# One bias table with reversed queries, table transfers on GpSimd's queue, and six raw weight tiles in a two-layer decoder trunk

## The chip, the cores and the metric

The kernel runs on one core of a Trainium2 chip. The engines are TensorE (PE; its weight loads are PEld), VectorE (DVE), ScalarE (ACT), GpSimd (POOL) and SyncE (SP), each of which works through its own list of instructions in order. The metric is the device time of one execution in microseconds (us), as the median of several.

## What is computed

A trunk of two layers on 256 tokens of 1024 channels, all in float32. The first layer mixes tokens by differential attention, the second by a diagonal state space model (SSM) with a gated output. Around each mixer stand two half-weighted feed-forward parts (FFN), and at the end a gated embedding (PLE). Every part has a norm in front and one behind.

```python
def reference(x, p, norm_g, ...):
    for i in range(DEPTH):
        g = norm_g[i]
        x = x + 0.5 * rmsnorm(swiglu(rmsnorm(x, g[0]), ffn_w_in[i, 0], ffn_w_out[i, 0]), g[1])
        h = rmsnorm(x, g[2])
        if i % 2 == 0:
            m = diff_attention(h, ..., rel_bias, lambda_init)
        else:
            m = s5_glu(h, ...)
        x = x + rmsnorm(m, g[3])
        x = x + 0.5 * rmsnorm(swiglu(rmsnorm(x, g[4]), ffn_w_in[i, 1], ffn_w_out[i, 1]), g[5])
        gate = sigmoid(rmsnorm(x, g[6]) @ ple_w_gate[i])
        x = x + rmsnorm(gate * (p[i] @ ple_w_proj[i]), g[7])
    return x

# in diff_attention, for a block of 128 queries and all keys:
    dist = q_pos[:, None] - k_pos[None, :]
    bias = rel_bias[t5_bucket(dist)]              # one value per softmax map and distance
    s = einsum('bhmqd,bhmkd->bhmqk', q_blk, k) + bias
    s = where(dist >= 0, s, NEG_INF)
    prob = softmax(s)
    attn = prob[:, :, 0] - lam * prob[:, :, 1]
```

## The kernel before

The 256 tokens are two blocks of 128, each a thread of Python generators whose steps alternate (block 0 leads by some steps). All weights are streamed once: 332 tiles of 128 x 1024 floats (512 KB) go from DRAM to a "raw" slot. ScalarE rounds a raw tile to float32r (hi, L131), VectorE takes the rest (lo, L133), and each product is three float32r matmuls (L302 to L304). The class `Weights` issues the loads on SyncE's queue (L119); a raw slot comes free once lo is done, and a pair of hi and lo once both blocks have used it. There are three raw slots and nine pairs (NB).

The order of each engine's list is written by the framework's scheduler, which goes by priorities and its own estimates. The calls `high_priority` and `issue_after` steer it, and the numbers in `OPT` say where.

Early in the program the attention bias is prepared (L525 to L540). A table of 16 softmax maps by 384 distances is filled by GpSimd and written to DRAM 128 times, once for each query of a block, by eight DMAs on SyncE's queue (L539). A read whose row stride is one less than a copy (L581) gives each query its own shift.

From the end of attention on, tables for the SSM are made between the other work, in eight groups gp (L908 to L948). GpSimd forms products vr, vi and or, oi (L897 to L902). TensorE transposes and multiplies them (v_ps, m_ps and m2_ps, L923 to L936), and SyncE stores them to v_d and o_d. The last parts are the diagonal terms db and dg (L952 to L959), the Toeplitz rows in m_d (L961) and their copy in t_d from DRAM to DRAM (L964, L965), all on SyncE's queue. GpSimd also computes the norms' factors: v is the sum of squares and r its power of -1/2 (L313 to L317). In names of norms the last digit is the block: r_pnple01 is the post norm of the first layer's PLE for block 1, and r_pre101 the norm in front of the second layer's first FFN for that block.

Of the kernel before, what the change touches and what calls it, by code (L numbers as in the profile page):

```python
# [9 lines left out]
F32 = mybir.dt.float32  # L10
# [6 lines left out]
P = 128  # L17
# [5 lines left out]
# Places in the schedule, by layer (f01: block 0, second ffn) or by norm (block, norm, token half).  # L23
# [49 lines left out]
def bucket_ranges(n_buckets=32, max_dist=128, n=256):  # L73
    """[start, stop) of the distances in each causal T5 bucket."""
    exact = n_buckets // 2
    of = []
    for d in range(n):
        if d < exact:
            of.append(d)
        else:  # L80
            large = exact + int(math.log(d / exact) / math.log(max_dist / exact) * (n_buckets - exact))
            of.append(min(large, n_buckets - 1))
    return [(of.index(b), n - of[::-1].index(b)) for b in range(n_buckets)]


class Weights:
    """Streams weight tiles [128, 1024] from DRAM and splits each into two float32r parts, or takes two tiles unsplit."""

    def __init__(self, nc, raw_pool, split_pool, specs):
# [8 lines left out]
        self.raws = 3  # L98
# [24 lines left out]
    def flush(self, force):  # L123
        """Splits what is loaded, up to the limit."""
        nc = self.nc
# [17 lines left out]
def trunk(ctx, tc, x, p, norm_g, ffn_w_in, ffn_w_out, attn_w_qkv, attn_w_o, attn_lam, attn_subln_g,  # L143
# [5 lines left out]
    raw_pool = ctx.enter_context(tc.tile_pool(name="raw", bufs=3))  # L149
# [11 lines left out]
    def extra_banks(name):  # L161
        """The last two banks serve one section after another."""
# [130 lines left out]
    def after_transposes(b, key, left):  # L293
        """The second block's last products of a layer leave room for the first block's transposes of the next."""
# [67 lines left out]
    def post_norm(b, halves, gain, factor, name):  # L362
        """x += factor * rmsnorm(m) with m in two [128, 512] PSUM banks."""
# [28 lines left out]
    def two_halves(b, accs, hi, lo, units, key):  # L392
        """Products over k into both halves; the last units finish the first half before the second."""
# [122 lines left out]
    if any(st[0] == "attn" for st in stages):  # L516
# [7 lines left out]
        # bias of every softmax map by j = key - query + 127 (distance 255 - j), masked beyond 255  # L524
# [11 lines left out]
        # one copy per query: a stride of one less than a copy then shifts the table by the query  # L536
        tab_d = dram.tile([P, 16, 384], F32, name="tab_d")
        for j in range(8):
            nc.sync.dma_start(tab_d[16 * j:16 * j + 16].rearrange("r m j -> m r j"),  # L539
                              tab.rearrange("m (o j) -> m o j", o=1).broadcast_to([16, 16, 384]))  # L540
# [34 lines left out]
    def scores(b, h):  # L575
# [4 lines left out]
        src = tab_d[0, 2 * h:2 * h + 2, 127 + 256 - nk:127 + 256 - nk + 1]  # L580
        nc.sync.dma_start(bias[:, :, 0:nk], bass.AP(tensor=src.tensor, offset=src.offset,  # L581
                                                      ap=[[16 * 384 - 1, P], [384, 2], [1, nk]]))
# [34 lines left out]
    def attention(b, qkv_units, pj_units, o_units):  # L617
# [9 lines left out]
        def normed(grp, on):  # L627
# [11 lines left out]
            for h in range(4):  # L639
                nc.tensor.transpose(pt[:, h * P:(h + 1) * P], on[:, h, :], ident)  # L640
            split_T(pt, oT_hi[:, grp * 4:grp * 4 + 4, :].rearrange("p a t -> p (a t)"),
                    oT_lo[:, grp * 4:grp * 4 + 4, :].rearrange("p a t -> p (a t)"), sub_g)
# [8 lines left out]
        for n, (part, grp) in enumerate(QKV_ORDER):  # L651
# [21 lines left out]
            if part == 0:  # L673
                for m in range(2):
                    (nc.vector.tensor_copy if m >= OPT["qz"] else nc.scalar.copy)(
                        qz[b][64 * m:64 * m + 64, :, m, :], ptv[64 * m:64 * m + 64])
# [41 lines left out]
    def exact_exp(out_, in_, n, nm):  # L718
        """exp to float32 accuracy: 2^(m / 16) times a short series of the rest."""
# [14 lines left out]
    def ssm_exp():  # L734
        """lambda, lambda * dt and the moduli |a|^k with states (e, p) on partitions, columns (q, g'): group 16q + 2g' + e."""
# [20 lines left out]
    def ssm_tables(pool, keep):  # L756
# [7 lines left out]
        # sine and cosine of lambda_im * dt: reduced to [-pi, pi], polynomials of the half angle  # L764
# [24 lines left out]
        # powers of a = rho e^(i theta), then of the phase and of the modulus by squaring  # L789
# [16 lines left out]
        # phases of a^(8j), moduli of a^8  # L806
# [23 lines left out]
        # (a - 1) / lambda  # L830
# [23 lines left out]
        # the norm's gain of the input channels goes into b and d  # L854
# [11 lines left out]
        # output matrices with states on partitions  # L866
# [39 lines left out]
        nc.sync.dma_start(m_d[:, :, 0:7, :].rearrange("i g k o -> i g (k o)"),  # L906
# [42 lines left out]
        # skip connection on the diagonal, Toeplitz rows to DRAM behind seven zero blocks  # L949
        m16 = msb.rearrange("p g e q h -> p (g e q) h")  # L950
        for q in range(4):
            db = pool.tile([16, 16, 16], F32, tag="cn", name=f"db{q}", bufs=1)  # L952
            nc.sync.dma_start(db, ssm_d[:, 256 * q:256 * q + 256].rearrange("o (g h) -> o g h", h=16).broadcast_to([16, 16, 16]))
            dg = pool.tile([16, 16, 16], F32, tag="vi", name=f"dg{q}", bufs=1)
            nc.sync.dma_start(dg, norm_g[1, 2:3, 256 * q:256 * q + 256].rearrange("o (g h) -> o g h", h=16).broadcast_to([16, 16, 16]))
# [5 lines left out]
        for k in range(8):  # L961
            nc.sync.dma_start(m_d[:, :, 7 + k, :], m16[16 * k:16 * k + 16])
        yield 2
        for s_ in range(8):  # L964
            nc.sync.dma_start(t_d[16 * s_:16 * s_ + 16].rearrange("i g (c x) -> i (g c) x", x=P),  # L965
# [4 lines left out]
    def ssm_u(b):  # L970
        """x and the norm's factors to the layout (channel group, block) x (step, channel) through DRAM."""
# [35 lines left out]
    def ssm_core(pool, vs, tos):  # L1007
# [35 lines left out]
        def grouped(out_ap, st_, w, **flags):  # L1043
            """One product per channel group: 32 stationary columns and 128 moving columns each."""
# [288 lines left out]
```

## Time and profile before

| What | Value |
|---|---|
| median of 3 runs | 1148.12 us (1147.39 to 1149.25) |
| profiled execution, span from its first to its last instruction | 1145.0 us |
| what lies around the span (median less span) | 3.1 us |
| TensorE busy | 1049.3 us, 92% |
| VectorE / ScalarE / GpSimd busy | 694.8 / 554.4 / 241.3 us |
| moved by DMA | 221.74 MB, mean 194 GB/s |

Times are of one profiled execution. A line as L131 is line 131 of the kernel before. Busy time of TensorE is modelled at its end and includes pipelining, so the number of its instructions in a window tells more of its pace than the share of time. A wait is put down to what came last.

### The profile page before, as it was taken

What the parts mean: (1) busy time and instruction counts of PE and PEld (TensorE: products, weight loads), DVE (VectorE), ACT (ScalarE), POOL (GpSimd) and SP (SyncE); (2) the same over time, 40 slices, a digit from 0 to 9 for tenths busy, and PEclk for the clock granted to TensorE, in tenths of its full rate; (3) what the DMA queues carried; (4) which work ended last, traced back from release to release, by engine and by line L of the source; (5) the groups of instructions that cost most, each with busy time, mean ns of one, the idle gap of its engine ahead of it and who ended that gap; (6) DMA issues with size and microseconds to landing.
All of it is one profiled execution on the core that took longest, in us unless ns stands there. A gap on an engine that the chain in (4) does not pass through costs nothing.

```text
span 1145.0 us, 14323 instructions
## 1 busy us (share of the span) xinstructions
PE 1049.3 (92%) x5123; PEld 839.2 (73%) x5123; DVE 694.8 (61%) x1011; ACT 554.4 (48%) x873; POOL 241.3 (21%) x289
## 2 busy tenths in 40 slices
PE   6599999999998999999787997999966999999997
PEld 4478888878776787777665776888744878888885
DVE  5166554659838897555678563655358576555464
ACT  5255444556765544443455542544343465444454
POOL 6000000000012004888889400000122010000001
PEclk9799999999999999999998998999987999999999
DMA  8976655646439667666556579756693557564651
GB/s 219 163 246 210 186 189 192 200 145 211 157 128 207 181 192 203 202 206 223 176 165 198 142 204 308 236 200 208 207 358 137 172 178 220 184 186 170 211 168 56
DMA packets 138103, 221.74 MB, mean 194 GB/s; under 512 B 34352, under 2 KB 63024, under 8 KB 138032
## 3 DMA queue, kind: packets, MB, share of 16 engines
q1 hardware_dynamic: 136976, 220.17, 62.8%
q8 instruction: 40, 0.66, 0.2%
q10 hardware_dynamic: 1056, 0.66, 0.2%
q14 instruction: 31, 0.25, 0.1%
HBM read 205.13 MB, written 19.86 MB: 196 GB/s over the span
## 4 chain that ended last, share of the span: by engine, by line
PE 48%; issue 19%; POOL 11%; DMA 9%; DVE 6%; ACT 4%; SPq 3%; DVEq 0%; POOLq 0%; ACTq 0%
PE up L302 7%; PE up L303 7%; PE up L304 7%; DMA raw<-in_ffn_w_in_dram 5%; PE dn L304 4%; PE dn L302 4%; PE dn L303 4%; DVE lo L133 2%; PE qkvat L302 2%; PE qkvat L303 2%; PE qkvat L304 2%; ACT hi L131 2%; POOL or L899 1%; PE sp L586 1%; DMA db<-in_ssm_d_dram 1%
## 5 line engine op out<-in xcount | busy, mean ns | idle before, releaser
L133 DVE TENSOR_TENSOR lo<-raw,hi 128x1024 fp32r<-128x1024 f32 x332 | 425.0, 1286 | 292.3 <-ACT hi L131 289.7
L131 ACT CAST hi<-raw 128x1024 fp32r<-128x1024 f32 x332 | 347.7, 1051 | 349.0 <-DMA raw<-in_ffn_w_in_dram 121.0
L302 PE MATMUL up<-hi,xThi 128*128 128x512 f32 x704 | 281.7, 403 | 22.5 <-ACT sg L444 8.9
L303 PE MATMUL up<-lo,xThi 128*128 128x512 f32 x704 | 280.3, 400 | 2.4 <-DVE lo L133 2.4
L304 PE MATMUL up<-hi,xTlo 128*128 128x512 f32 x704 | 281.6, 405 | 0.0
L302 PEld LDWEIGHTS up<-hi,xThi 128*128 128x128 f32 x704 | 135.5, 193 | 52.8 <-ACT sg L444 9.8
L303 PEld LDWEIGHTS up<-lo,xThi 128*128 128x128 f32 x704 | 135.3, 192 | 33.0 <-DVE lo L133 5.0
L304 PEld LDWEIGHTS up<-hi,xTlo 128*128 128x128 f32 x704 | 135.1, 193 | 29.2 <-issue 0.8
L302 PE MATMUL dn<-hi,hThi 128*128 128x512 f32 x352 | 138.3, 394 | 0.0
L304 PE MATMUL dn<-hi,hTlo 128*128 128x512 f32 x352 | 138.1, 393 | 0.0
L303 PE MATMUL dn<-lo,hThi 128*128 128x512 f32 x352 | 138.0, 392 | 0.0
L313 POOL TENSOR_SCALAR v_pn<-sspn,sspn 128x1 f32<-128x1 f32 x8 | 3.4, 423 | 359.9 <-ACT junkpn L370 356.9
L304 PEld LDWEIGHTS dn<-hi,hTlo 128*128 128x128 f32 x352 | 66.4, 189 | 14.1 <-issue 0.4
L303 PEld LDWEIGHTS dn<-lo,hThi 128*128 128x128 f32 x352 | 66.4, 189 | 13.9 <-DVE lo L133 0.2
L302 PEld LDWEIGHTS dn<-hi,hThi 128*128 128x128 f32 x352 | 66.4, 189 | 13.6 <-issue 0.2
L321 ACT ACTIVATE xThi<-xT_ps,gT 128x128 fp32r<-128x128 f32 x112 | 38.9, 366 | 48.7 <-PE xT_ps L339 48.4
L326 DVE TENSOR_TENSOR hTlo<-hT_ps,hThi 128x512 fp32r<-128x512 f32 (+1 forms) x48 | 30.8, 643 | 36.6 <-ACT hThi L325 36.6
L325 ACT CAST hThi<-hT_ps 128x512 fp32r<-128x512 f32 (+1 forms) x48 | 26.4, 549 | 53.2 <-PE hT_ps L449 53.1
L322 DVE SCALAR_TENSOR_TENSOR xTlo<-xT_ps,gT,xThi 128x128 fp32r<-128x128 f32 x112 | 36.5, 344 | 20.5 <-ACT xThi L321 20.2
L339 PE MATMUL xT_ps<-ident,x 128*128 128x128 f32 x112 | 31.1, 300 | 17.7 <-DVE xTlo L322 10.7
L444 ACT ACTIVATE sg<-up,r_pre 128x512 f32<-128x512 f32 (+1 forms) x48 | 30.8, 650 | 20.9 <-PE up L304 11.5
L446 DVE SCALAR_TENSOR_TENSOR h<-up,r_pre,sg 128x512 f32<-128x512 f32 (+1 forms) x48 | 33.6, 701 | 11.0 <-ACT sg L444 8.5
(352 smaller groups left out, 1296.4 us busy)
## 6 DMA issues: line engine op xcount, KB each, us to landing
raw<-in_ffn_w_in_dram SPq DMA_DIRECT2D x160, 512.0 KB, 4.4
raw<-in_ffn_w_out_dram SPq DMA_DIRECT2D x88, 512.0 KB, 3.9
raw<-in_attn_w_qkv_dram SPq DMA_DIRECT2D x24, 512.0 KB, 4.3
raw<-in_ffn_w_in_dram SPq DMA_DIRECT2D x32, 256.0 KB, 3.5
raw<-in_ple_w_gate_dram SPq DMA_DIRECT2D x16, 512.0 KB, 4.3
raw<-in_ssm_w_glu_dram SPq DMA_DIRECT2D x16, 512.0 KB, 4.2
gain<-in_norm_g_dram SPq DMA_DIRECT2D x8, 512.0 KB, 4.8
raw<-in_attn_w_o_dram SPq DMA_DIRECT2D x8, 512.0 KB, 4.0
```

The lines of the kernel that those rows point to most:

```text
L131: nc.scalar.copy(hi, raw)
L133: (nc.gpsimd if n in self.on_pool else nc.vector).tensor_tensor(lo, raw, hi.bitcast(F32), ALU.subtract)
L302: nc.tensor.matmul(out_ap, st_hi, w_hi, start=start, stop=False)
L303: nc.tensor.matmul(out_ap, st_hi, w_lo, start=False, stop=False)
L304: nc.tensor.matmul(out_ap, st_lo, w_hi, start=False, stop=stop)
L321: return (nc.scalar.activation(hi, psum, AF.Copy, scale=scale).ins, nc.vector.scalar_tensor_tensor(lo, psum, scale, hi.bitcast(F32), ALU.m ...
L322: nc.vector.scalar_tensor_tensor(lo, psum, scale, hi.bitcast(F32), ALU.mult, ALU.subtract).ins)
L325: nc.scalar.copy(hi, psum)
L326: nc.vector.tensor_tensor(lo, psum, hi.bitcast(F32), ALU.subtract)
L339: marks[b].append(nc.tensor.transpose(pt, xb[:, k * P:(k + 1) * P], ident).ins)
L444: nc.scalar.activation(sg[:, :w], gp, AF.Silu, scale=r)
L446: nc.vector.scalar_tensor_tensor(h[:, :w], up_, r, sg[:, :w], ALU.mult, ALU.mult)
```

## The change

There are four parts. The bias table is written to DRAM once, by a DMA on GpSimd's queue. Queries are reversed when they are copied out of PSUM (query 127 comes first), so that a row stride of plus one in that single table gives each query its shift; the attention output is turned back where it is split for the next product. The zero blocks of m_d, the diagonal terms db and dg, the rows of m_d and the copies to t_d are issued by GpSimd and no longer by SyncE. The raw slots are six in place of three, and the limit on loads that wait for their split goes with them. The scratch that the framework reserves for DMA descriptors is 4096 bytes of a partition, which makes room for three more slots of 4096 bytes.

Comment lines are left out too, so line numbers from L25 to L540 are one higher in the changed kernel, and those from about L541 on one lower.

```diff
+RAWS = 6
...
-        self.raws = 3
+        self.raws = RAWS
...
-    raw_pool = ctx.enter_context(tc.tile_pool(name="raw", bufs=3))
+    raw_pool = ctx.enter_context(tc.tile_pool(name="raw", bufs=RAWS))
...
-        tab_d = dram.tile([P, 16, 384], F32, name="tab_d")
-        for j in range(8):
-            nc.sync.dma_start(tab_d[16 * j:16 * j + 16].rearrange("r m j -> m r j"),
-                              tab.rearrange("m (o j) -> m o j", o=1).broadcast_to([16, 16, 384]))
+
+        tab_d = dram.tile([16, 384], F32, name="tab_d")
+        nc.gpsimd.dma_start(tab_d, tab)
...
-        src = tab_d[0, 2 * h:2 * h + 2, 127 + 256 - nk:127 + 256 - nk + 1]
+        src = tab_d[2 * h:2 * h + 2, 256 - nk:256 - nk + 1]
         nc.sync.dma_start(bias[:, :, 0:nk], bass.AP(tensor=src.tensor, offset=src.offset,
-                                                      ap=[[16 * 384 - 1, P], [384, 2], [1, nk]]))
+                                                      ap=[[1, P], [384, 2], [1, nk]]))
...
-            split_T(pt, oT_hi[:, grp * 4:grp * 4 + 4, :].rearrange("p a t -> p (a t)"),
-                    oT_lo[:, grp * 4:grp * 4 + 4, :].rearrange("p a t -> p (a t)"), sub_g)
+            split_T(pt.rearrange("p (a t) -> p a t", a=4)[:, :, ::-1], oT_hi[:, grp * 4:grp * 4 + 4, :],
+                    oT_lo[:, grp * 4:grp * 4 + 4, :], sub_g)
...
-                        qz[b][64 * m:64 * m + 64, :, m, :], ptv[64 * m:64 * m + 64])
+                        qz[b][64 * m:64 * m + 64, :, m, :], ptv[64 * m:64 * m + 64, :, ::-1])
...
-        nc.sync.dma_start(m_d[:, :, 0:7, :].rearrange("i g k o -> i g (k o)"),
+        nc.gpsimd.dma_start(m_d[:, :, 0:7, :].rearrange("i g k o -> i g (k o)"),
...
-            nc.sync.dma_start(db, ssm_d[:, 256 * q:256 * q + 256].rearrange("o (g h) -> o g h", h=16).broadcast_to([16, 16, 16]))
+            nc.gpsimd.dma_start(db, ssm_d[:, 256 * q:256 * q + 256].rearrange("o (g h) -> o g h", h=16).broadcast_to([16, 16, 16]))
...
-            nc.sync.dma_start(m_d[:, :, 7 + k, :], m16[16 * k:16 * k + 16])
+            nc.gpsimd.dma_start(m_d[:, :, 7 + k, :], m16[16 * k:16 * k + 16])
...
-            nc.sync.dma_start(t_d[16 * s_:16 * s_ + 16].rearrange("i g (c x) -> i (g c) x", x=P),
+            nc.gpsimd.dma_start(t_d[16 * s_:16 * s_ + 16].rearrange("i g (c x) -> i (g c) x", x=P),
...
-    nc = _bacc.Bacc("TRN2", target_bir_lowering=False, num_devices=1)
+    nc = _bacc.Bacc("TRN2", target_bir_lowering=False, num_devices=1, dynamic_dma_scratch_size=4096)
```

Three places show how the lists move. In names, the first digits behind "raw" are the weight tile's number, and the last number is a buffer's.

SyncE's list in the first FFN, before: the eight writes of the table (L539) stand between the weight tiles 6 to 9.

```order
L359 DMA gain01_1251<-in_norm_g_dram 128x1024
L119 DMA raw3_290<-in_ffn_w_in_dram 128x2x512
L119 DMA raw4_296<-in_ffn_w_in_dram 128x2x512
L119 DMA raw5_302<-in_ffn_w_in_dram 128x2x512
L119 DMA raw6_308<-in_ffn_w_in_dram 128x2x512
L539 DMA tab_d_172<-tab_138 16x16x384 x3
L119 DMA raw7_314<-in_ffn_w_in_dram 128x2x512
L539 DMA tab_d_172<-tab_138 16x16x384 x2
L119 DMA raw8_320<-in_ffn_w_in_dram 128x2x512
L539 DMA tab_d_172<-tab_138 16x16x384 x3
```

The same stretch after the change:

```order
L120 DMA raw5_295<-in_ffn_w_in_dram 128x2x512
L541 DMA lam_b_174<-in_attn_lam_dram 128x256
L553 DMA sub_g_185<-in_attn_subln_g_dram 128x1
L360 DMA gain01_1244<-in_norm_g_dram 128x1024
L120 DMA raw6_301<-in_ffn_w_in_dram 128x2x512
L120 DMA raw7_307<-in_ffn_w_in_dram 128x2x512
L120 DMA raw8_313<-in_ffn_w_in_dram 128x2x512
L120 DMA raw9_400<-in_ffn_w_in_dram 128x2x512
L120 DMA raw10_418<-in_ffn_w_in_dram 128x2x512
L120 DMA raw11_436<-in_ffn_w_in_dram 128x2x512
```

The table's writes are gone from it, and tile 5 is loaded ahead of the first gain.

GpSimd's list around block 1's post norm of the first layer's PLE, before: r_pnple01 comes one product after v_pnple01.

```order
L898 TENSOR_TENSOR ptv7_4827<-ai_3143,bi_3630 128x512
L313 TENSOR_SCALAR v_pnple01_5624<-sspnple010_5618,sspnple011_5621 128x1
L897 TENSOR_TENSOR vr7_4825<-ar_3142,br_3629 128x512
L317 TENSOR_TENSOR r_pnple01_5626<-v_pnple01_5624,neg_half_92 128x1
L900 TENSOR_TENSOR vi7_4826<-ai_3143,br_3629 128x512
L899 TENSOR_TENSOR vr7_4825<-vr7_4825,ptv7_4827 128x512
L901 TENSOR_TENSOR ptv7_4827<-ar_3142,bi_3630 128x512
L315 TENSOR_SCALAR v_pre101_5661<-ss101_5659 128x1
L902 TENSOR_TENSOR vi7_4826<-vi7_4826,ptv7_4827 128x512
L317 TENSOR_TENSOR r_pre101_5663<-v_pre101_5661,neg_half_92 128x1
```

After the change, with the transfers in it:

```order
L901 TENSOR_TENSOR oi7_4898<-oi7_4898,pto7_4899 128x512
L952 DMA db0_4946<-in_ssm_d_dram 16x256
L314 TENSOR_SCALAR v_pnple01_5617<-sspnple010_5611,sspnple011_5614 128x1
L961 DMA m_d_106<-msb_3809 1024x1x16 x7
L318 TENSOR_TENSOR r_pnple01_5619<-v_pnple01_5617,neg_half_92 128x1
L954 DMA dg0_4948<-in_norm_g_dram 16x256
L954 DMA dg1_4955<-in_norm_g_dram 16x256
L316 TENSOR_SCALAR v_pre101_5654<-ss101_5652 128x1
L952 DMA db1_4953<-in_ssm_d_dram 16x256
L318 TENSOR_TENSOR r_pre101_5656<-v_pre101_5654,neg_half_92 128x1
L954 DMA dg2_4962<-in_norm_g_dram 16x256
```

Between v_pnple01 and r_pnple01 there are now seven writes of m_d, of 1024 pieces each, and the loads of dg and db stand around v_pre101.

TensorE's list where the last group of tables (v_ps70, m_ps7) begins, before: block 1's x has been transposed in part (xT_ps1010), and the second layer's first FFN (up) is under way.

```order
L304 MATMUL up10000_5520<-hi177_5523,xTlo100_5484 128x512
L304 MATMUL up10001_5593<-hi181_5596,xTlo100_5484 128x512
L339 MATMUL xT_ps1010_5632<-ident_87,x1_96 128x128
L302 MATMUL up10000_5520<-hi177_5523,xThi100_5483 128x512
L303 MATMUL up10000_5520<-lo177_5524,xThi100_5483 128x512
L302 MATMUL up10001_5593<-hi181_5596,xThi100_5483 128x512
L303 MATMUL up10001_5593<-lo181_5597,xThi100_5483 128x512
L339 MATMUL xT_ps1011_5633<-ident_87,x1_96 128x128
L304 MATMUL up10000_5520<-hi177_5523,xTlo100_5484 128x512
L304 MATMUL up10001_5593<-hi181_5596,xTlo100_5484 128x512
L923 MATMUL v_ps70_4839<-ident_87,vr7_4825 128x128
L930 MATMUL m_ps7_4854<-vr7_4825,cp0_3817 32x128 x4
```

After the change:

```order
L303 MATMUL gtple010_5386<-hi171_5290,xThi061_5351 128x512
L304 MATMUL gtple010_5386<-lo171_5291,xThi061_5351 128x512
L303 MATMUL gtple011_5387<-hi171_5290,xThi061_5351 128x512
L304 MATMUL gtple011_5387<-lo171_5291,xThi061_5351 128x512
L922 MATMUL v_ps70_4832<-ident_87,vr7_4818 128x128
L929 MATMUL m_ps7_4847<-vr7_4818,cp0_3810 32x128 x4
L340 MATMUL xT_ps0611_5354<-ident_87,x1_96 128x128
L305 MATMUL gtple010_5386<-hi171_5290,xTlo061_5352 128x512
L305 MATMUL gtple011_5387<-hi171_5290,xTlo061_5352 128x512
L340 MATMUL xT_ps1000_5478<-ident_87,x0_94 128x128
L922 MATMUL v_ps70_4832<-ident_87,vi7_4819 128x128
L922 MATMUL v_ps70_4832<-ident_87,vr7_4818 128x128
```

The last group is now among the PLE's products (gtple) of block 1, ahead of block 1's transposes. From the first v_ps50 to m2_ps7 there are 189 rows, where there were 271, and from m2_ps7 to the first xT_ps1010 there are 29 rows, 26 of them matmuls and 3 transposes.

## Rows read from the trace of the kernel before

**Rows 1.** Page, busy time by engine, then the chain that ended last:

```profile
PE 1049.3 (92%) x5123; PEld 839.2 (73%) x5123; DVE 694.8 (61%) x1011; ACT 554.4 (48%) x873; POOL 241.3 (21%) x289
...
PE 48%; issue 19%; POOL 11%; DMA 9%; DVE 6%; ACT 4%; SPq 3%; DVEq 0%; POOLq 0%; ACTq 0%
```

**Rows 2.** Windows: start:end, length, busy per engine (xinstructions), clock, DMA share, GB/s:

```profile
0.00:25.00 25.00, 15.72 (x57) 10.43 (x58) 15.00 (x44) 14.20 (x27) 14.01 (x54) 1.00 0.79 236
25.00:100.00 75.00, 59.65 (x244) 47.61 (x243) 32.50 (x39) 29.91 (x35) 3.87 (x1) 0.86 0.84 204
100.00:225.00 125.00, 125.00 (x569) 103.26 (x567) 69.16 (x69) 58.06 (x70) 0.86 (x2) 1.00 0.60 190
350.00:375.00 25.00, 20.93 (x89) 14.87 (x88) 19.98 (x69) 12.08 (x25) 5.06 (x9) 0.93 0.92 200
450.00:550.00 100.00, 93.72 (x487) 73.03 (x486) 55.02 (x44) 43.94 (x59) 86.48 (x66) 1.00 0.67 211
650.00:725.00 75.00, 65.78 (x284) 52.45 (x283) 36.19 (x44) 28.26 (x34) 1.33 (x2) 0.95 0.82 243
```

**Rows 3.** Waits, 0 to 100 us: us in total, times, longest:

```profile
ACT hi L131 <- DMA raw<-in_ffn_w_in_dram: 37.0, 21, 10.2
```

**Rows 4.** Timeline of SyncE's queue: start, duration of the issues, what:

```profile
20.21 4.22 SPq L539 DMA_DIRECT2D tab_d<-tab  x3
...
28.37 7.70 SPq L539 DMA_DIRECT2D tab_d<-tab  x2
...
36.88 8.28 SPq L539 DMA_DIRECT2D tab_d<-tab  x3
```

**Rows 5.** Windows, work on the raw weight tiles alone:

```profile
25.00:50.00 25.00, 2.45 (x2) 2.10 (x2) 0.83 0.91 138
50.00:75.00 25.00, 10.97 (x9) 9.45 (x9) 0.82 0.85 242
75.00:100.00 25.00, 12.28 (x11) 11.22 (x11) 0.93 0.75 231
100.00:225.00 125.00, 55.48 (x46) 47.49 (x46) 1.00 0.60 190
```

**Rows 6.** Issues by line (last: median us to landing), and page groups (last busy, mean ns):

```profile
raw<-in_ffn_w_in_dram SPq DMA_DIRECT2D x160, 512.0 KB, 4.4
...
L133 DVE TENSOR_TENSOR lo<-raw,hi 128x1024 fp32r<-128x1024 f32 x332 | 425.0, 1286 | 292.3 <-ACT hi L131 289.7
L131 ACT CAST hi<-raw 128x1024 fp32r<-128x1024 f32 x332 | 347.7, 1051 | 349.0 <-DMA raw<-in_ffn_w_in_dram 121.0
```

**Rows 7.** Waits, 340 to 380 us:

```profile
ACT hi L131 <- DMA raw<-in_ffn_w_in_dram: 8.0, 4, 4.2
```

**Rows 8.** SyncE's queue, 650 to 700 us:

```profile
652.05 3.49 SPq L962 DMA_DIRECT2D m_d<-msb  x4
...
684.17 11.52 SPq L965 DMA_DIRECT2D t_d<-m_d  x8
```

**Rows 9.** Chain of waits, 655 to 705 us: start, us, what:

```profile
671.20 3.54 DMA db<-in_ssm_d_dram
...
695.78 7.91 DMA raw<-in_ffn_w_in_dram
```

**Rows 10.** DMA queues, kinds, MB, share of 16 engines:

```profile
q1 hardware_dynamic: 136976, 220.17, 62.8%
q8 instruction: 40, 0.66, 0.2%
q10 hardware_dynamic: 1056, 0.66, 0.2%
```

**Rows 11.** TensorE timeline, first table transposes of groups 1 and 5, last of group 7:

```profile
470.72 0.33 PE L923 MATMUL v_ps<-ident,vr 128*128 128x128 f32 x1 [0.43 <-POOL vr L899]
...
571.48 0.27 PE L923 MATMUL v_ps<-ident,vr 128*128 128x128 f32 x1
...
646.78 0.27 PE L936 MATMUL m_ps<-ident,mt 128*128 128x128 f32 x1
```

More of the change, by code (lines that the diff above doesn't have):

```diff
@@ L952, in ssm_tables @@
             db = pool.tile([16, 16, 16], F32, tag="cn", name=f"db{q}", bufs=1)
-            nc.sync.dma_start(db, ssm_d[:, 256 * q:256 * q + 256].rearrange("o (g h) -> o g h", h=16).broadcast_to([16, 16, 16]))
+            nc.gpsimd.dma_start(db, ssm_d[:, 256 * q:256 * q + 256].rearrange("o (g h) -> o g h", h=16).broadcast_to([16, 16, 16]))
             dg = pool.tile([16, 16, 16], F32, tag="vi", name=f"dg{q}", bufs=1)
-            nc.sync.dma_start(dg, norm_g[1, 2:3, 256 * q:256 * q + 256].rearrange("o (g h) -> o g h", h=16).broadcast_to([16, 16, 16]))
+            nc.gpsimd.dma_start(dg, norm_g[1, 2:3, 256 * q:256 * q + 256].rearrange("o (g h) -> o g h", h=16).broadcast_to([16, 16, 16]))
             v.tensor_tensor(db, db, dg, ALU.mult)
```

## The prediction

> **What bounds the kernel now.** I read the busy shares and the chain first. The reader is to see that TensorE is busy in 92% of the span and leads the chain of waits with 48%, while the chain's next parts are issue time, POOL (GpSimd) with 11% and DMA with 9% [rows 1]. So what can be won is the time in which TensorE has nothing to do, and the next view is the table of windows [rows 2]. From 100 to 225 us TensorE runs 569 matrix instructions in 125 us, 4.55 per us, without a pause: that is the pace to which I hold the rest. From 25 to 100 us there are 244 where the pace allows 341, so 97 are missing, worth 21 us. From 350 to 375 us TensorE is idle for 4.1 us, and from 650 to 725 us there are 284 instructions instead of 341, worth 12.5 us. DMA is 82 to 92% busy in these three windows and 60% in the steady one.
>
> Who is late at the start: ScalarE's casts waited 37.0 us for weight tiles in the first 100 us [rows 3]. The SyncE queue shows why. Between 20 and 45 us the eight writes of the bias table hold its issue for 4.22 + 7.70 + 8.28 = 20.2 us, and the weight loads are queued between and behind them [rows 4]. Between 25 and 50 us only 2 tiles were cast; once the writes are over it is 11 in 25 us, 2.3 us each, and in the steady stretch 46 in 125 us, 2.7 us each [rows 5]. The supply is thus quicker than the demand when nothing stands in its way. It is also bound by its slots: a raw tile is held for landing, cast and subtraction, 4.4 + 1.05 + 1.29 = 6.7 us [rows 6], so three slots give a tile each 2.25 us at best.
>
> **The change part by part.** The sum is made against the span of 1145.0 us; the timed median of 1148.12 is 3.1 us above it, and that is added at the end.
>
> A, the single table. Eight writes of 16 x 16 x 384 floats (3.1 MB) become one of 16 x 384, and it leaves SyncE's queue. The weight loads that stood behind 20.2 us of issue go out at once, up to six ahead. The gain is at most the 21 us of missing instructions from 25 to 100 us, plus up to 5 us of the first window, where TensorE was idle for 9.3 us [rows 2] and the very first inputs take part of that in any case. From below it is the transfer time of the 3.1 MB alone, 12.7 us at the 242 GB/s of the window from 50 to 75 us [rows 5]. I take 20, near the upper figure, since the steady pace shows that TensorE needs nothing else than tiles. The reversed query order leaves the number and size of all copies and splits as they were, they only read PSUM backwards; each bias read has as many pieces as before, now all from one 24 KB region. For both together I take 0, bounds -1 and +2: TensorE's other work covers a small difference.
>
> B, six slots at the first layer change. There casts waited 8.0 us in four waits for weights [rows 7], while SyncE loads the small tables of the state space layer. With three more tiles loaded ahead most of that is covered: I take 3 of the 4.1 us idle, bounds 0 and 5.
>
> C, table transfers off SyncE's queue at 650 to 725 us. On SyncE the seven writes of m_d and the eight of t_d took 3.49 us for four and 11.52 us for eight [rows 8], and the weight tile issued behind them was on the chain with 7.91 us instead of 4.4 [rows 6, 9]. After the change SyncE goes on with weights, but the 8 MB that t_d reads and writes still pass the same DMA engines. That the tile needed 7.91 us shows this contention, so I take 7 of the 12.5 us; bounds 0 and 12.5. The Trainium skill's page "DMA: Bandwidth & Descriptors", section "Issuing engines are not separate DMA queues", says that moving a DMA to another engine's queue saves the sequencer's time and not the transfer's. The 7.91 us agree with it; by that rule alone C would be nearer to its lower half, some 4 us.
>
> D, the same transfers on POOL. This is the part that can cost. POOL's list now has, between v_pnple01 and r_pnple01 (the factor of block 1's post norm), seven writes of m_d with 1024 pieces each. Block 1's x, and with it the transposes that TensorE has next in its order, wait for r_pnple01. Before, it stood behind one table product. TensorE has 26 matmuls between the last table transpose (m2_ps7) and those transposes, 5.7 us; about 1.7 us of that go to the factor itself and the update of x, so 4 us are cover. No row of the trace shows a DMA issued by POOL: the list of queues has the hardware kind and instruction fetch alone [rows 10]. The nearest rows are SyncE's issues: 3.49 / 4 = 0.87 us for the same m_d write, 11.52 / 8 = 1.44 us for t_d, also 1024 pieces, and 7.70 / 2 = 3.85 us for the dearest, the table writes with the queue full [rows 4, 8]. I take 1.44, the dearer of the two with as many pieces: 7 x 1.44 - 4 = 6 us of stall. Bounds: 0 (POOL isn't held at all) and 7 x 3.85 - 4 = 23. Behind it come the four pairs dg/db, now on POOL too, each of which waits for DVE's work on the last pair, and DVE's list has block 1's splits and the next weight tiles' subtractions between these. Three rounds of issue (1.44), landing (3.54 us [rows 9]) and 1 us of DVE are 18 us; TensorE has about 60 instructions, 13 us, up to there, so some 5 us stick out, of which I take 3 since the rounds begin early; bounds 0 and 8. D together +9, bounds 0 and 31. The one write of zeros costs nothing: POOL waited for that transfer before as well.
>
> The Trainium skill's same page, section "SWDGE vs HWDGE vs iDMA", says that descriptors of a DMA issued by GpSimd are computed by software on its cores, while SyncE's come from hardware. No run here shows it. By its section "Anatomy of one DMA", which calls that generation small and variable, D would be near 3 us and the time near 1121; if the software pays for each piece, it is the first rival below.
>
> E, the order of the table products. TensorE's list is packed closer: from the first v_ps50 to m2_ps7 there are 189 rows where there were 271. Before, these 271 took 646.78 - 571.48 = 75.3 us, where 60 would do at the pace, so some 15 were lost. POOL is busy for 86.5 of 100 us in this section [rows 2], with one group each (571.48 - 470.72) / 4 = 25.2 us [rows 11], so 21.8 us of work. Two groups, and the some 11 us from v_ps70 to m2_ps7, need 55 us, and 189 rows at the pace 41: 14 are lost. The two losses are alike; I count 0, bounds -5 and +8.
>
> The smaller scratch only makes the room for the three slots: 0.
>
> Sum: -20 - 3 - 7 + 9 + 0 = -21, a span of 1124 and a time of 1127 us. Its own range is 1114 to 1139.
>
> **The rivals.**
> First, POOL's issue becomes the wait, and the kernel slower. Place: r_pnple01 behind the seven writes. All else sums to -20 - 3 - 7 + 3 - 4 = -31 us, so the sides change at 31 / 7 = 4.4 us for one issue, and it is measurably slower from 4.8 us. At 5.5 us it would be 1145 - 31 + 38.5 + 3.1 = 1156 us. For it: 1024 pieces each on a path that no row shows. Against it: even SyncE's issue into a full queue was 3.85 us.
>
> Second, the six slots do nothing and only the start counts, because the nine pairs of split tiles (NB = 9) and not the raw slots hold the loads; B and C vanish: 1145 - 20 + 9 + 3 = 1137 us. For it: SyncE's loads mostly wait on DVE in the steady stretch, where TensorE lacks nothing. Against it: in the windows that lose time casts wait for DMA, not for room.
>
> Third, more is won: POOL's issue is cheap (D 0), C gives 12 us, A its 25 and B 3: 1145 - 40 + 3 = 1108 us. For it: the steady pace shows that nothing but supply is missing. Against it: t_d's bytes stay.
>
> **How the numbers follow.** Likeliest 0.53, first rival 0.13, second 0.14, third 0.20. A measurement of this kernel can tell 0.2% from no change, 2.3 us. Faster is the likeliest, the third, and nearly all of the second, with a part for POOL's dear end: 0.84. Slower is nearly all of the first, 0.12, and 0.04 lie between. The range takes in the third rival at the low end and D's bound of 23 us at the high end, where the sum is near -4: 1107 to 1147, which leaves out the first rival and some of the third.
>
> **What would show it.** Right for A: TensorE's window from 25 to 100 us has some 335 instructions, and casts don't wait there; wrong if they still wait for DMA at 30 us. Right for B and C: TensorE idle under 2 us at the first layer change, and over 310 instructions in the 75 us behind m2_ps7. For D the duration of the m_d issues on POOL's queue decides, and the time between v_pnple01 and r_pnple01: near 10 us by my value, near 35 for the first rival. The whole is wrong if the start gains under 12 us or if block 1's transposes stand still for over 25 us.

## The result and the profile after

The changed kernel takes 1133.65 us (median of 4 runs, 1132.87 to 1135.29) where the kernel before takes 1148.68 us beside it: a ratio of 0.9871, 95% interval 0.9852 to 0.989. The forecast was 1127 us in a range of 1107 to 1147. The profiled execution has a span of 1131.0 us, 14.0 less than before; forecast were 21 less.

The windows of the changed kernel answer to [rows 2]. The fourth is the first layer change, which lies 20 us earlier than before. Columns: start:end, length, busy time of PE, PEld, DVE, ACT, POOL (xinstructions), granted clock, DMA share, GB/s.

```profile
0.00:25.00 25.00, 17.36 (x63) 12.18 (x64) 15.26 (x37) 16.33 (x28) 12.51 (x50) 1.00 0.94 341
25.00:100.00 75.00, 72.86 (x333) 59.28 (x332) 44.71 (x58) 37.52 (x45) 9.40 (x6) 1.00 0.67 199
100.00:225.00 125.00, 124.43 (x565) 101.82 (x564) 69.11 (x80) 60.26 (x84) 3.68 (x10) 1.00 0.56 177
330.00:355.00 25.00, 19.39 (x84) 14.23 (x82) 20.80 (x79) 10.92 (x24) 7.89 (x7) 0.93 0.87 193
450.00:550.00 100.00, 92.90 (x462) 72.82 (x461) 56.62 (x41) 41.37 (x57) 82.33 (x65) 0.97 0.63 197
610.00:635.00 25.00, 14.87 (x58) 10.52 (x57) 9.31 (x19) 8.97 (x19) 14.38 (x19) 0.83 0.56 139
650.00:725.00 75.00, 74.93 (x345) 61.74 (x344) 42.48 (x42) 36.78 (x42) 6.61 (x9) 1.00 0.82 280
```

The start runs at the steady pace: 333 instructions from 25 to 100 us, where there were 244. The 75 us from 650 on are full too, 345 in place of 284. But between 610 and 635 us TensorE is busy for only 14.9 of 25 us.

SyncE's queue at the start answers to [rows 4] (columns: start, duration of the issues, what):

```profile
2.65 5.14 SPq L120 DMA_DIRECT2D raw<-in_ffn_w_in_dram  x4
8.72 0.34 SPq L541 DMA_DIRECT2D lam_b<-in_attn_lam_dram  x1
10.77 0.34 SPq L553 DMA_DIRECT2D sub_g<-in_attn_subln_g_dram  x1
11.15 0.43 SPq L360 DMA_DIRECT2D gain<-in_norm_g_dram  x1
12.18 13.73 SPq L120 DMA_DIRECT2D raw<-in_ffn_w_in_dram  x9
```

The table's writes are gone from it. Of the casts' waits for weights in the first 100 us, 37.0 us in [rows 3], one is left (columns: us in total, times, longest):

```profile
ACT hi L132 <- DMA raw<-in_ffn_w_in_dram: 0.6, 1, 0.6
```

GpSimd's list around block 1's post norm in the changed kernel; the bracket at a row's end is the idle time ahead of it and what ended it:

```profile
616.68 0.61 POOL L952 DMA_DIRECT2D db<-in_ssm_d_dram  x1 [2.01 <-DMA o_d<-or]
617.38 0.95 POOL L314 TENSOR_SCALAR v_pnple<-sspnple,sspnple 128x1 f32<-128x1 f32 x1
618.39 2.34 POOL L961 DMA_DIRECT2D m_d<-msb  x3
624.32 2.27 POOL L961 DMA_DIRECT2D m_d<-msb  x3 [3.59 <-issue]
628.19 0.77 POOL L961 DMA_DIRECT2D m_d<-msb  x1 [1.60 <-issue]
628.97 0.60 POOL L318 TENSOR_TENSOR r_pnple<-v_pnple,neg_half 128x1 f32<-128x1 f32 x1
```

One issue takes 2.34 / 3 = 0.78 us. After three of them GpSimd stands still for 3.59 us, after six for 1.60 us. From v_pnple01 to r_pnple01 it is 11.6 us. VectorE and TensorE wait for it (waits from 600 to 640 us), and TensorE's next products after the wait last longer (its timeline: start, duration, what):

```profile
DVE x L378 <- POOL r_pnple L318: 8.5, 1, 8.5
...
PE xT_ps L340 <- DVE x L378: 6.9, 1, 6.9
```

```profile
630.40 0.69 PE L340 MATMUL xT_ps<-ident,x 128*128 128x128 f32 x2 [6.91 <-DVE x L378]
...
632.42 0.63 PE L303 MATMUL up<-hi,xThi 128*128 128x512 f32 x1
632.84 0.63 PE L304 MATMUL up<-lo,xThi 128*128 128x512 f32 x1
...
637.00 0.39 PE L305 MATMUL up<-hi,xTlo 128*128 128x512 f32 x1
637.23 0.39 PE L303 MATMUL up<-hi,xThi 128*128 128x512 f32 x1
```

**Where the time went.** I numbered TensorE's weight products (L303 to L305, 3984 of them, 12 for each of the 332 tiles) by their start in each trace and subtracted the start of the same number before. Where tables are mixed in, the order differs a little, so the middle columns are good to some 2 us. Each trace is also a single execution, which lies up to 2.9 us from its kernel's median (the most for the five slots). The columns are the product's number and, under it, its start before; each entry is us earlier (-) or later (+) than before at that point.

```
                              780    1380    2220    2460    3900
start before                220.0   405.7   653.3   723.3  1115.7
changed kernel              -20.3   -17.9    +0.7   -12.2   -14.1
bias table alone            -15.1   -13.5   -11.7   -11.0   -11.6
six slots alone              -3.4    -1.7    +9.0    -4.0    -6.7
all transfers on SyncE      -20.1   -18.4    -7.6   -19.3   -22.8
m_d, db, dg on SyncE        -20.2   -19.4    -7.1   -20.3   -24.4
three slots, 16 KB scratch  -13.3   -12.2    -7.3   -12.4   -13.3
three slots, 4 KB scratch   -13.7   -13.3    -9.3   -12.7   -12.7
five slots, all on SyncE    -15.7   -14.6    -6.9   -10.9   -14.8
m_d's rows on SyncE         -20.1   -18.7   -11.4   -24.6   -27.9
three of m_d on GpSimd      -20.3   -17.7    -9.5   -22.0   -24.3
m_d and t_d on SyncE        -20.5   -18.3   -10.9   -22.1   -26.8
tables every third step     -20.1   -16.3    -3.9   -17.0   -21.2
```

The changed kernel wins 20.3 us up to product 780, gives back 2.4 by 1380 and 18.6 more by 2220, and wins 12.9 again by 2460. The rows below its own are the experiments.

### The profile page after: what moved, and what is told of

The parts are those of the page before. It is cut to its first block, busy times and chain, and to the rows that moved or that the text cites. A ratio compares the mean times of both kernels' runs of the same rounds, so it can differ in the third digit from the quotient of the medians.

```text
span 1131.0 us, 14367 instructions
## 1 busy us (share of the span) xinstructions
PE 1047.9 (93%) x5123; PEld 839.1 (74%) x5123; DVE 696.3 (62%) x1011; ACT 553.4 (49%) x873; POOL 260.7 (23%) x315
## 5 line engine op out<-in xcount | busy, mean ns | idle before, releaser
L134 DVE TENSOR_TENSOR lo<-raw,hi 128x1024 fp32r<-128x1024 f32 x332 | 430.2, 1305 | 242.5 <-ACT hi L132 237.3
L303 PE MATMUL up<-hi,xThi 128*128 128x512 f32 x704 | 279.7, 399 | 5.8 <-ACT xThi L322 4.0
L305 PE MATMUL up<-hi,xTlo 128*128 128x512 f32 x704 | 279.8, 403 | 0.8 <-DVE xTlo L323 0.8
L303 PEld LDWEIGHTS up<-hi,xThi 128*128 128x128 f32 x704 | 134.2, 191 | 34.6 <-ACT xThi L322 6.6
L305 PEld LDWEIGHTS up<-hi,xTlo 128*128 128x128 f32 x704 | 133.5, 191 | 31.2 <-DVE xTlo L323 1.6
L303 PE MATMUL dn<-hi,hThi 128*128 128x512 f32 x352 | 139.0, 395 | 0.0
L305 PE MATMUL dn<-hi,hTlo 128*128 128x512 f32 x352 | 137.5, 391 | 0.0
L305 PEld LDWEIGHTS dn<-hi,hTlo 128*128 128x128 f32 x352 | 66.4, 189 | 14.1 <-issue 0.2
L303 PEld LDWEIGHTS dn<-hi,hThi 128*128 128x128 f32 x352 | 66.5, 189 | 13.8 <-ACT hi L132 0.2
L340 PE MATMUL xT_ps<-ident,x 128*128 128x128 f32 x112 | 30.8, 301 | 18.2 <-DVE xTlo L323 10.1
L303 PE MATMUL qkvat<-hi,xThi 128*128 128x512 f32 x96 | 38.8, 404 | 0.2 <-ACT xThi L322 0.2
```

Of the source, the lines that this page charges most:

```text
L134: (nc.gpsimd if n in self.on_pool else nc.vector).tensor_tensor(lo, raw, hi.bitcast(F32), ALU.subtract)
L303: nc.tensor.matmul(out_ap, st_hi, w_hi, start=start, stop=False)
L305: nc.tensor.matmul(out_ap, st_lo, w_hi, start=False, stop=stop)
L340: marks[b].append(nc.tensor.transpose(pt, xb[:, k * P:(k + 1) * P], ident).ins)
```

## Experiments

Times are medians; since the kernel before itself moved from 1147.4 to 1151.0 us between the chips used, runs of different groups are compared by their ratio to it.

**1. The bias table alone.** The kernel before with the new table and the reversed queries:

```diff
-        tab_d = dram.tile([P, 16, 384], F32, name="tab_d")
-        for j in range(8):
-            nc.sync.dma_start(tab_d[16 * j:16 * j + 16].rearrange("r m j -> m r j"),
...
+        tab_d = dram.tile([16, 384], F32, name="tab_d")
+        nc.gpsimd.dma_start(tab_d, tab)
```

> The kernel before with the single bias table and the reversed queries alone: three raw slots, the state space transfers on SyncE, the scratch as before. Theory (the ledger of the two traces): the first 100 us gain 20 us from the table alone, whatever the slots, and nothing else changes: 1128 to 1131 us. Rival: the loads need the six slots to run ahead, so the table alone gives only the 12.7 us of its transfer: 1135 to 1138 us.

Measured: 1132.96 us, ratio 0.9869 (0.985 to 0.9887). The table alone wins 15.1 us at the start, so both were off: most of the 20 us comes with the table, the last 5 need the slots. In total it does as much as the whole change (0.9871): what the other parts win and lose cancels.

**2. The slots alone.** The kernel before with these lines:

```diff
-        self.raws = 3
+        self.raws = 6
...
-    raw_pool = ctx.enter_context(tc.tile_pool(name="raw", bufs=3))
+    raw_pool = ctx.enter_context(tc.tile_pool(name="raw", bufs=6))
...
-    nc = _bacc.Bacc("TRN2", target_bir_lowering=False, num_devices=1)
+    nc = _bacc.Bacc("TRN2", target_bir_lowering=False, num_devices=1, dynamic_dma_scratch_size=4096)
```

> The kernel before with six raw slots and the small scratch alone. Theory: SyncE's 20 us of table writes stay, so the start gains at most 2 us; the closer order of the table products costs about 7 us between 400 and 560 us, and the three tiles loaded ahead take back some of the stall at 690 to 710 us: 1144 to 1153 us. Rival: the slots are what gives most of the gain of the start: under 1138 us.

Measured: 1140.2 us, ratio 0.9937 (0.9921 to 0.9952), below the range of the theory. At the start it wins 3.4 us, a little more than the 2 expected. What I had too low is the stretch behind product 2220: there it wins 13.0 us (+9.0 to -4.0), as much as the changed kernel (12.9), with m_d and t_d still on SyncE. So the slots are enough for that gain.

**3 and 4. The transfers back on SyncE.** The changed kernel with, first, all of GpSimd's state space transfers on SyncE, then all but t_d:

```diff
-            nc.gpsimd.dma_start(m_d[:, :, 7 + k, :], m16[16 * k:16 * k + 16])
+            nc.sync.dma_start(m_d[:, :, 7 + k, :], m16[16 * k:16 * k + 16])
```

and the same at the zeros, db, dg and (first kernel only) t_d.

> The changed kernel with the zeros, db, dg, m_d and t_d issued by SyncE again. Theory: r_pnple01 no longer stands behind the writes of m_d, so block 1's x comes about 9 us earlier; the stall at 690 to 710 us comes back in part, since SyncE's weight loads stand behind m_d and t_d, but three more tiles are loaded: 6 to 10 us lost there. Together 1129 to 1136 us. Rival 1: the six slots cover that stall, and the transfers cost nothing on SyncE: 1122 to 1126 us. Rival 2: the move to GpSimd is what wins the 13 us behind 660 us and costs little itself: 1139 to 1146 us.

> The changed kernel with the zeros, db, dg and m_d issued by SyncE again, t_d still by GpSimd. Theory: the stall of TensorE for block 1's x comes from the seven writes of m_d ahead of r_pnple01 and goes with them (9 us), while the weight loads pass t_d as in the changed kernel: 1124 to 1128 us. Rival: the stall is that of the table products and of the closer order, and m_d on GpSimd has little to do with it: 1131 to 1136 us.

Measured: 1123.95 us, ratio 0.9793 (0.9776 to 0.9811), and 1123.54 us, ratio 0.9793 (0.9774 to 0.9812). My theory of the first was too high and its first rival right: with six slots the transfers cost little on SyncE. The second is half a microsecond below the theory and far from its rival. Both are alike, so t_d's queue is worth nothing that can be told, and by the ratios the move to GpSimd costs the changed kernel some 9 us.

**5. m_d's eight writes alone on SyncE** (one line of the diff above):

> The changed kernel with the eight writes of m_d's rows alone on SyncE; zeros, db, dg and t_d stay on GpSimd. Theory: the seven writes ahead of r_pnple01 are the whole loss, r_pnple01 ends some 2 us after v_pnple01 starts instead of 12 us, and the time is that of the run with all but t_d on SyncE: 1122 to 1126 us. Rival: the db and dg rounds around v_pre101 cost 3 us or more by themselves: 1127 to 1131 us.

Measured: 1119.82 us, ratio 0.9738 (0.9709 to 0.9768), the fastest kernel of the study and below the theory. GpSimd's list in it, to set beside that of the changed kernel:

```profile
614.75 0.61 POOL L952 DMA_DIRECT2D db<-in_ssm_d_dram  x1 [1.88 <-DMA o_d<-or]
615.46 1.08 POOL L314 TENSOR_SCALAR v_pnple<-sspnple,sspnple 128x1 f32<-128x1 f32 x1
616.62 0.57 POOL L318 TENSOR_TENSOR r_pnple<-v_pnple,neg_half 128x1 f32<-128x1 f32 x1
617.16 0.58 POOL L954 DMA_DIRECT2D dg<-in_norm_g_dram  x1
```

From v_pnple01 to r_pnple01 it is 1.2 us instead of 11.6, and the loss between products 1380 and 2220 is 7.3 us instead of 18.6. So the seven writes cost 11.3 us there; over the whole span it is 13.8 us (1131.0 to 1117.2).

**6 and 7. The scratch.** The changed kernel with three slots, once with 16384 bytes of scratch (as before the change) and once with 4096. The lists of all engines are equal in the two. Both have the first edit, the first of them the second as well:

```diff
-RAWS = 6
+RAWS = 3
...
-    nc = _bacc.Bacc("TRN2", target_bir_lowering=False, num_devices=1, dynamic_dma_scratch_size=4096)
+    nc = _bacc.Bacc("TRN2", target_bir_lowering=False, num_devices=1)
```

> The changed kernel with three raw slots and the scratch of 16384 bytes as before; all table transfers stay on GpSimd, where r_pnple01 now stands ahead of the writes of m_d. It differs from the first experiment (the bias table alone, 1132.96 us) by GpSimd's transfers. Theory: the gain behind 660 us came from the six slots and not from SyncE's freedom, so nothing is gained here: 1130 to 1135 us. Rival, as the prediction had it: SyncE's freedom alone wins 7 us there: 1123 to 1128 us. On the scratch: the gaps of 1.3 to 5.9 us between GpSimd's issues of m_d and t_d come from the small scratch and are absent here (eight issues in some 7 us).

> As the run with three raw slots and 16384 bytes, but with a scratch of 4096 bytes; every engine's list is the same. Theory: the small scratch holds three such transfers, so gaps of 1 to 6 us stand behind the third issue of m_d and of t_d, which delays the last t_d by 10 to 15 us, and the time is the same within 2 us, since t_d is needed only 150 us later. Rival: the gaps are the queue's own pace, and both runs show them alike.

Measured: 1133.28 us, ratio 0.9843 (0.9819 to 0.9866), and 1133.88 us, ratio 0.9852 (0.983 to 0.9875). GpSimd's issues of m_d and t_d with 16384 bytes, then with 4096:

```profile
639.25 5.30 POOL L961 DMA_DIRECT2D m_d<-msb  x7
...
679.66 6.02 POOL L964 DMA_DIRECT2D t_d<-m_d  x8 [3.98 <-DMA m_d<-msb]
```

```profile
637.34 2.30 POOL L961 DMA_DIRECT2D m_d<-msb  x3
642.80 0.76 POOL L961 DMA_DIRECT2D m_d<-msb  x1 [3.16 <-issue]
643.93 0.75 POOL L961 DMA_DIRECT2D m_d<-msb  x1 [0.37 <-issue]
645.75 0.75 POOL L961 DMA_DIRECT2D m_d<-msb  x1 [1.06 <-issue]
648.55 0.77 POOL L961 DMA_DIRECT2D m_d<-msb  x1 [2.05 <-issue]
```

With the large scratch seven issues stand back to back in 5.30 us; with the small one the same seven take 12.0 us (637.34 to 649.32), with a stop after the third. The stops are the small scratch's. Here they cost no time, since r_pnple01 stands ahead of m_d in these lists. And with three slots SyncE's freedom moves the ratio from 0.9869 (experiment 1) to 0.9843, less than the intervals tell apart: the rival, that SyncE's freedom alone makes the kernel 7 us faster, is out. Behind product 2220 that freedom does win something, though: 5.1 and 3.4 us here, where the table alone loses 0.7. These two kernels lose about as much elsewhere, 4.9 and 4.0 us between 1380 and 2220 (the table alone 1.8) and some 1.5 at the start.

**8. Three of the seven writes on GpSimd.** Experiment 5 with one part turned back:

```diff
-            nc.sync.dma_start(m_d[:, :, 7 + k, :], m16[16 * k:16 * k + 16])
+            (nc.gpsimd if k in (1, 2, 3) else nc.sync).dma_start(m_d[:, :, 7 + k, :], m16[16 * k:16 * k + 16])
```

> As the run with m_d's eight writes on SyncE (1119.82 us), but three of the seven that are ready early go back to GpSimd, again between v_pnple01 and r_pnple01; every other instruction of GpSimd's list stays. Theory: the scratch holds three, so there is no gap behind them and r_pnple01 comes only 3 x 0.77 = 2.3 us later: 1120 to 1124 us. Rival 1: each write costs the same share of the 13.8 us, 5.9 us for three: 1125 to 1128 us. Rival 2: any write of m_d there waits for its data and drags the whole stall in: over 1130 us.

Measured: 1123.14 us, ratio 0.978 (0.9757 to 0.9803). Ahead of r_pnple01 there are now 2.34 us of issue and no stop:

```profile
615.71 1.14 POOL L314 TENSOR_SCALAR v_pnple<-sspnple,sspnple 128x1 f32<-128x1 f32 x1
616.91 2.34 POOL L961 DMA_DIRECT2D m_d<-msb  x3
619.25 0.60 POOL L318 TENSOR_TENSOR r_pnple<-v_pnple,neg_half 128x1 f32<-128x1 f32 x1
```

The time is within the theory's range, and in the products it lies 1.9 us behind experiment 5 at number 2220 and 3.6 at 3900. By the ratios alone (4.8 us from experiment 5, with intervals that overlap) the first rival, 5.9 us, isn't far off; the list and the products at 2220 speak for the theory, without deciding it. The second rival is out.

**9. t_d on SyncE as well.** Experiment 5 with

```diff
-            nc.gpsimd.dma_start(t_d[16 * s_:16 * s_ + 16].rearrange("i g (c x) -> i (g c) x", x=P),
+            nc.sync.dma_start(t_d[16 * s_:16 * s_ + 16].rearrange("i g (c x) -> i (g c) x", x=P),
```

> As the run with m_d's eight writes on SyncE (1119.82 us), but the eight copies to t_d on SyncE as well; only the zeros, db and dg stay on GpSimd. Theory: with six slots SyncE's 12 us of t_d issues are covered by tiles loaded ahead, so t_d's queue is worth nothing and the db and dg loads, which wait for VectorE, are the only part worth moving: 1118 to 1122 us. Rival, as the prediction had it: t_d on SyncE holds the weight loads and costs some 5 to 7 us behind 640 us: 1124 to 1128 us.

Measured: 1121.0 us, ratio 0.9754 (0.9731 to 0.9776), as the theory said, and not to be told from experiment 5. What a free SyncE is worth with six slots is thus the zeros, db and dg: 0.9754 against 0.9793 in experiment 3, some 4 us, though the intervals touch. The trace of experiment 3 shows where: VectorE waits for the second db, which SyncE issues among its writes of m_d, and TensorE waits for block 1's xTlo, which stands behind that in VectorE's list (VectorE's row, then TensorE's):

```profile
625.00 0.41 DVE L955 TENSOR_TENSOR db<-db,dg 16x256 f32<-16x256 f32 x1 [3.73 <-DMA db<-in_ssm_d_dram]
```

```profile
626.63 0.48 PE L340 MATMUL xT_ps<-ident,x 128*128 128x128 f32 x1 [3.43 <-DVE xTlo L323]
```

With db and dg on GpSimd (experiments 5 and 9) this wait of TensorE is gone. There that xTlo stands ahead of the second db in VectorE's list, so it is not shown whether the queue or that order wins the 4 us.

**10. Five slots.** Experiment 3 (all transfers on SyncE) with

```diff
-RAWS = 6
+RAWS = 5
```

> The changed kernel with the state space transfers back on SyncE and five raw slots. TensorE's list then has the tables in the order of the kernel before (235 rows from the first v_ps50 to m2_ps7, not 189). Theory: six slots cost some 5 us between 400 and 650 us by the closer order of the tables, which five slots don't, while the start and the stretch behind 660 us want four or more slots: 1117 to 1123 us. Rival: the order of the tables costs nothing by itself, and the sixth slot counts: 1124 to 1129 us.

Measured: 1129.55 us, ratio 0.9811 (0.9785 to 0.9838). The theory fails, and the rival, that the sixth slot counts, is 0.6 us off. Against experiment 3 the kernel wins 4.4 us less at the start, and behind product 2220 it wins 4.0 us and not 11.7. Between 1380 and 2220 it loses 7.7 us and not 10.8. By the ratios alone the two are not told apart (0.9811 and 0.9793), and the traced execution of five slots is its slowest. Its order of the tables lies between the two others and isn't that of the kernel before: from the first v_ps50 to m2_ps7 there are 235 rows, where there were 271 before and 189 with six slots.

**11. A looser order of the tables.** Experiment 5 with

```diff
- 'every': 2,
+ 'every': 3,
```

> As the run with m_d's eight writes on SyncE (1119.82 us), with a step of the tables in every third step of block 1's thread in place of every second, which spreads TensorE's table rows out again (220 rows from the first v_ps50 to m2_ps7 in place of 189). Theory: the some 4 us that six slots lost between 390 and 670 us are waits of TensorE for GpSimd's products in the closer order (14 us of waits), so the looser order wins 2 to 5 us: 1115 to 1118 us. Rival: GpSimd's own chain of eight groups sets that section, whatever TensorE's order: 1118 us or more.

Measured: 1125.76 us, ratio 0.9794 (0.9769 to 0.9819), slower than experiment 5: the theory fails, and the rival is right in its number. TensorE's waits from 380 to 680 us, in experiment 5 and then here:

```profile
PE v_ps L922 <- POOL vi L901: 14.2, 8, 4.9
...
PE xT_ps L340 <- DVE x L378: 0.6, 1, 0.6
```

```profile
PE xT_ps L340 <- DVE x L378: 12.3, 3, 6.4
PE v_ps L922 <- POOL vi L901: 7.2, 5, 2.1
```

The waits for GpSimd's products halve, and those for the updated x grow by 11.7 us. One wait is traded for a dearer one.

## Why the prediction was right in sign and time, and where it was not

**A, the start: right.** I took 20 us near the upper bound, and it is 20.3. The way there was right as well: casts that waited 37.0 us now wait 0.6. Not seen was that the table alone gives 15.1 and the slots alone 3.4 (experiments 1 and 2); the rest needs both. A slip that changed nothing: 3.1 MB at 242 GB/s are 13 us and not 12.7.

**B, the first layer change: wrong, by 5 us.** I took a gain of 3; the products lose 2.4 between 780 and 1380, and TensorE is idle for 5.6 of the 25 us there, where I had said under 2. The casts no longer wait for weights there ([rows 7] had 8.0 us). The step that failed is that nothing else was late: TensorE's waits of the changed kernel from 320 to 365 us name others.

```profile
PE xT_ps L340 <- DVE xTlo L323: 3.2, 2, 3.0
PE c_psre L876 <- DMA cnre<-in_ssm_c_re_dram: 1.8, 1, 1.8
```

Every other run loses there too, 0.4 to 3.8 us: the table alone with its three slots 1.6, the slots alone 1.7. So the slots make no difference that shows, and what causes the small loss stays open.

**C, behind 650 us: the size too small and the cause wrong.** I took 7 us, bound 12.5, for taking m_d and t_d off SyncE. It is 12.9, and six slots alone give 13.0 with both transfers on SyncE. TensorE's wait for casts of weights from 640 to 740 us, in the kernel before, then with three slots and a free SyncE (experiment 6), then with five slots and the transfers on SyncE (experiment 10):

```profile
PE up L302 <- ACT hi L131: 6.1, 1, 6.1
```

```profile
PE up L303 <- ACT hi L132: 3.6, 2, 3.0
```

```profile
PE up L303 <- ACT hi L132: 4.0, 2, 2.9
```

With six slots TensorE has no such wait, in the changed kernel and in experiment 2 alike. So tiles loaded ahead of the transfers remove the stall, whichever queue the transfers are on; a free queue with three slots removes a part of it. The Trainium skill's page "DMA: Bandwidth & Descriptors", section "Issuing engines are not separate DMA queues", which I cited for a small C, says that such a move saves only the time of issuing. With six slots t_d agrees: its issues hold SyncE for 11.48 us in experiment 9, and the time is as in experiment 5 within what can be told.

**D, the writes of m_d: the place right, the size too small, and one cost left out.** Block 1's x did come late by r_pnple01 behind the seven writes. I took 9 us in all; the seven writes alone measure 11.3. An issue costs 0.78 us and not 1.44, so the issues alone are 5.4 us. But I costed the small scratch at nothing, and it stops GpSimd for 3.59 + 1.60 = 5.2 us here: 10.6 us where I had 10.1, the right number by two errors. What came on top is TensorE after its wait. Its windows on both sides of the restart (columns as in the first fence):

```profile
610.00:625.00 15.00, 10.58 (x47) 7.51 (x45) 5.76 (x11) 5.34 (x13) 9.09 (x10) 1.00 0.72 210
625.00:635.00 10.00, 4.29 (x11) 3.01 (x12) 3.55 (x8) 3.63 (x6) 5.29 (x10) 0.57 0.32 31
```

In the ten microseconds around the restart the granted clock is 0.57, so mostly at 1.2 and not at 2.4 GHz. In experiment 5, where TensorE doesn't wait for x, it stays at 1.00 from 610 to 635 us. The products of 632 us start 0.42 us apart and those of 637 us 0.23 us; from 631.40 to 636.47 us it is a dozen at the slow level, 12 x 0.19 = 2.3 us. The wait of 6.9 us (I had 6) and these 2.3 are 9.2 of the 11.3; the rest stays open. The db and dg rounds, priced at 3 us, cost nothing: experiment 5 keeps them on GpSimd and is the fastest, and with them on SyncE the kernel is no faster (experiments 3 and 9).

**E, the order of the tables: wrong by 7 us.** I counted two losses as alike and took 0, bounds -5 and +8. It is +7.3, by experiment 5, where D is gone. The step that failed is the 55 us for the section from the first table transpose of group 5 to the last of group 7. It took 62.2 us (551.23 to 613.45), and the two groups in it 50.2 us where I had 43.6. The section's windows, before and then changed (columns as in the first fence):

```profile
571.48:647.05 75.57, 64.05 (x316) 47.26 (x315) 55.90 (x66) 42.90 (x83) 59.38 (x53) 0.93 0.56 173
551.23:613.78 62.55, 48.16 (x235) 34.30 (x235) 40.28 (x45) 30.82 (x60) 58.97 (x53) 0.84 0.56 170
```

GpSimd was busy for 59 us in both, so its work was more than the 55 us for which I took it, and it fills nearly all of the closer section. The sum also held rows against a pace of instructions: the 271 and 189 rows hold 313 and 231 instructions, 69 and 51 us at the pace. With that, 6.5 us were lost before and 11.4 now, 5 us more; the other 2 lie ahead of group 5. The closer order is not shown to be the cause, since of two looser ones five slots lose less than their like (7.7 against 10.8, experiments 10 and 3) and the third step loses more (12.4 against 7.3, experiment 11). What more slots do to this section stays open.

D and E together are measured, 18.6 us; how they divide depends on the run that stands for a kernel without D. Against experiment 3, with all transfers on SyncE, D is 7.8 us and E 10.8, which has the wait for db in it that experiment 9 tells of.

The sum by its steps: -20.3 + 2.4 + 7.3 + 11.3 - 12.9 makes -12.2, with -1.9 more in the state space core and behind, which I had not counted: -14.1, where the span is 14.0 less. Forecast was -20 - 3 + 0 + 9 - 7 = -21. B, E and D were some 15 us too good and C and the uncounted end some 8 too bad: that the time came out within 7 us is A's doing and, for the rest, partly luck.

**The rivals.** GpSimd's issue did become the wait, but at 0.78 us and not beyond the 4.4 us at which the sides change. That the six slots do nothing is refuted by experiment 2. The third, where D is 0 and C 12, is nearly what experiment 5 is: its ratio times the 1148.12 us of the forecast is 1118 us, where the rival had 1108, with E's loss still in it.

## What to carry to other kernels

Before a DMA is moved to GpSimd, look at what stands behind it in GpSimd's list, and count its stops as well as its issues: seven writes of 0.78 us became 10.6 us ahead of a factor of 0.6 us that TensorE waited for. A stall behind transfers can come from a queue that is held or from too little loaded ahead; trying each alone tells them apart: here six slots removed the stall with the queue still held, and a free queue with three slots only a part of it. Parts that win are best timed apart from parts that come with them: the bias table alone gives 0.9869, the whole change 0.9871, and the whole change with m_d's writes left on SyncE 0.9738.

## What had not been expected of the hardware

- A DMA of 1024 pieces is issued by GpSimd in 0.75 to 0.81 us; SyncE took 0.87 us for the same write of m_d [rows 8]. So in these runs GpSimd is no slower at issuing than SyncE. The page of the changed kernel lists it as one more queue beside those of [rows 10], as software (columns: packets, MB, share of 16 engines):

```profile
q0 software_dynamic: 1824, 5.33, 1.8%
```

- A scratch of 4096 bytes held three such DMAs; of m_d the fourth waited 3.16 us (experiment 7) and 3.59 us (changed kernel). With 16384 bytes seven and eight went out without a stop (experiment 6).
- Around TensorE's wait of 6.9 us the granted clock fell from 1.00 to 0.57 for 10 us, so that wait cost some 2.3 us more.
